# Second-block experts: wide expert swapped to place 28, with four edits around routing, constants and norm vectors

## The chip, the cores and the metric

The kernel runs on one core of one Trainium2 chip. The metric is the device time of one execution in microseconds; shown is the median of several executions. A profile of one more execution gives the trace. All times within it count from its first instruction.

## The reference

A sequence of 256 tokens of width 1024 passes two blocks, each a mixer with a residual and then a layer of experts with another. The first block's experts choose their tokens (16 experts, 32 tokens each). The change lies in and around the second block's experts. There each token chooses: four groups of eight experts, the best group by a softmax, in it the two best experts:

```python
top_logit, top_local = lax.top_k(e_logits, EXPERT_TOPK)       # 2 of 8, in the chosen group
expert = g_sel[:, None] * EXPERTS_PER_GROUP + top_local       # 0..31
hid = silu(xb @ gate[e]) * (xb @ up[e]);  y += weight * (hid @ down[e])
```

256 tokens with two experts each make 512 places for 32 experts, 16 on average; an expert may get any number. Each expert has a gate and an up matrix of 1024 x 256 and a down matrix of 256 x 1024, 1 MB each in float32. Before the experts stands a layer norm (ln1), after them a residual and another (ln2).

## The kernel before

The work runs as one program on five engines; a scheduler orders each engine's instructions by the order of the source and a cost model, and inserts the waits. `issue_after(ins)` keeps an instruction behind another one of the same engine in that order, without a wait.

**Constants.** `setup2` and `load_s5` (L754 to L766) load the second block's constants (p2, cf2, p2s; 1.9 MB together) while the first block's experts run. They are issued from ScalarE's queue. All other large loads are issued by SP (`load1`, `w`, `prefetch2`). DMAs of the SP and ScalarE queues share a small set of completion counters, given out in turn; a DMA that takes a counter waits until the counter's earlier DMA has landed.

**Rows and routing.** `mix_out` (L1588) ends the mixer: the output rows of the two halves of tokens (a = 0, 1), the norm's statistics, the logits, then `split_rows`. It scales a half in place on VectorE, copies it, rounded and with its columns reordered, to x3h on ScalarE, and GpSimd subtracts the two into x3l. `route_rows` is the chain of some ten small VectorE instructions that picks the two experts; its result is the mask Mk. `moe2_route` counts Mk up by matmuls with a triangle, which gives each token's place in its expert (pos), builds one-hot matrices of 32 places per expert and gathers the tokens of the first eight experts by matmul with x3h and x3l. `weights` (run at the start of `moe2_experts`) works out the weight of each pick (Wt).

**A block of 32 places, and one more.** Every expert gets one block of 32 places. An expert with more than 32 tokens is found in `weights`; its number goes to a register (xid), and a 33rd block "x" computes its places 33 to 64, with weights loaded once more. If any other expert has more than 32, or this one more than 64, `moe2_overflow` loops over all experts.

**Loads and slots.** `order2` writes out the order of the loads: in groups of four experts, first the gates and ups, then the downs; before the last group the three of block "x". `prefetch2` takes for each load the slot of SBUF that came free first (`k.free2`, 18 slots); at the end of group 6 `restore3` takes three of them for the norm vectors and for the sum `k.pre`. The norm vectors (ln1 and ln2, weight and bias) are four DMAs from GpSimd's queue that repeat one row of 4 KB on 128 partitions each.

**The groups.** `moe2_experts` runs g = 0 to 7: `gate_up` of two experts at a time, `turn` (transposes), `down` of the four experts of the group before, `scatter` (adds their rows to the four accumulators in PSUM). Block "x" goes in group 7. The tiles yh and yl between `down` and `scatter` exist once. Then `finish` normalises and writes the output.

Of the kernel before, what the change touches and what calls it, by code (L numbers as in the profile page):

```python
# [11 lines left out]
I32 = mybir.dt.int32  # L12
# [741 lines left out]
def setup2(k):  # L754
    nc = k.nc
    n = k.s5o
    both = k.cp2.tile([P, n + k.io["cf2"].shape[1]], F32, tag="w0", bufs=1, name="p2")
    k.p2, k.c2f = both[:, 0:n], both[:, n:]
    nc.scalar.dma_start(k.p2, k.io["p2"][:, 0:n])
    nc.scalar.dma_start(k.c2f, k.io["cf2"])  # L760


def load_s5(k):
    n, m = k.s5o, k.io["p2"].shape[1]
    k.p2s = k.s5t.tile([P, m - n], F32, name="p2s")
    k.nc.scalar.dma_start(k.p2s, k.io["p2"][:, n:m])  # L766
# [821 lines left out]
def mix_out(k):  # L1588
# [15 lines left out]
    k.x3T = k.xg.tile([P, 8, S], F32, tag="xi2", bufs=2, name="x3T")  # L1604
    k.lg = k.xg.tile([P, 2, 36], F32, name="lg")
# [53 lines left out]
    norm_rows(1, st[1])  # L1659
    split_rows(0, st[0])  # L1660
    route = route_rows(k)
# [58 lines left out]
def prefetch2(k, n):  # L1720

    for _ in range(n):
        e, name = ORDER2[len(k.loaded2)]
        nk = 2 if name == "down" else 8
        k.slot2[e, name] = slot = k.free2.pop(0)
        k.loaded2[e, name] = t = k.slot_tile(*slot, (P, nk, 2048 // nk))
        src = k.io[f"expert_w_{name}_2"].rearrange("e (p k) n -> e p k n", p=P)
        if e == E2:
            if name == "gate":
                k.more2 = k.nc.values_load(k.xid[0:1, 0:1], engines=(mybir.EngineType.SP,), min_val=0, max_val=E2 - 1)  # L1730
            k.nc.sync.dma_start(t, src[bass.ds(k.more2, 1)].rearrange("e p k n -> p (e k) n"))
        else:
            k.nc.sync.dma_start(t, src[e])
# [68 lines left out]
def moe2_route(k):  # L1802
# [10 lines left out]
    for a in range(2):  # L1813
# [5 lines left out]
        V.tensor_tensor(oh[:, a], io32(k), k.pos[:, a, 0:8, None].to_broadcast([P, 8, C2]), OP.is_equal)  # L1819
        for kk in range(8):  # L1820
            sl = slice((kk % 2) * 256, (kk % 2 + 1) * 256)
            for x in (k.x3h, k.x3l):
                T.matmul(pg[kk // 2][:, sl], x[:, a, kk * P:(kk + 1) * P], oh[:, a].rearrange("p e c -> p (e c)"),
                         start=(a + kk % 2 == 0 and x is k.x3h), stop=(a == 1 and x is k.x3l), skip_group_check=True)
            if a:
                gathered2(k, xi, kk, pg[kk // 2][:, sl])
    k.wt2 = Wt.rearrange("p a g e -> p a (g e)")
    ps = k.pj()
    T.matmul(ps[:, 0:32], one, mk[:, 0, :], start=True, stop=False)
    T.matmul(ps[:, 0:32], one, mk[:, 1, :], start=False, stop=True)  # L1830

    def weights():
# [12 lines left out]
        io = k.c1("iota")  # L1845
        many, big = (pool.tile([P, n], F32, name=nm) for n, nm in ((E2, "many"), (2, "big2")))
        pick = V.scalar_tensor_tensor(many, ps[:, 0:32], C2 + 0.5, io[:, 0:E2], OP.is_gt, OP.mult)
        V.tensor_reduce(big[:, 0:1], many, AX.X, OP.max)
        k.xid = pool.tile([1, 1], I32, name="xid")
        V.tensor_scalar(k.xid, big[0:1, 0:1], -1.0, 0.0, OP.add, OP.max)  # L1850
        k.px, k.wx = (pool.tile([P, 2], F32, name=nm) for nm in ("px", "wx"))
        for a in range(2):
            for d, v in ((k.px, k.pos), (k.wx, k.wt2)):
                V.scalar_tensor_tensor(many, io[:, 0:E2], big[:, 0:1], v[:, a], OP.is_equal, OP.mult, accum_out=d[:, a:a + 1])
        V.tensor_scalar(many, io[:, 0:E2], big[:, 0:1], float(C2), OP.is_equal, OP.mult)
        V.scalar_tensor_tensor(many, ps[:, 0:32], -float(C2), many, OP.add, OP.subtract)
        V.tensor_reduce(big[:, 1:2], many, AX.X, OP.max)
        k.over = pool.tile([1, 1], I32, name="over")
        V.tensor_scalar(k.over, big[0:1, 1:2], 0.5, None, OP.is_gt)
        k.big2 = big  # L1860

    k.weights2 = weights


def moe2_overflow(k):
# [5 lines left out]
    over = nc.values_load(k.over[0:1, 0:1], min_val=0, max_val=1)  # L1871
# [4 lines left out]
    with tc.If(over > 0):  # L1876
        V.memset(k.rone, 1.0)
        kept = pool.tile([P, 2, E2], F32, name="kept")
        for a in range(2):
            V.scalar_tensor_tensor(kept[:, 0], k.c1("iota")[:, 0:E2], k.big2[:, 0:1], k.pos[:, a], OP.is_equal, OP.mult)  # L1880
# [63 lines left out]
def moe2_experts(k):  # L1944
# [31 lines left out]
    def gather_more():  # L1976
# [4 lines left out]
        for a in range(2):  # L1981
            V.tensor_tensor(oh["x"][:, a], k.c1("iota")[:, C2:2 * C2], k.px[:, a:a + 1].to_broadcast([P, C2]), OP.is_equal)
            G.tensor_scalar(ow["x"][:, a], oh["x"][:, a].bitcast(F32), k.wx[:, a:a + 1], None, OP.mult)
# [10 lines left out]
    def gate_up(r):  # L1994
        es = (2 * r, 2 * r + 1) if r != "x" else (E2,)
        ws = [loaded2(k, e, "gate", "up") for e in es]
        ps = k.mx()
        for kk in range(8):
            for i in range(2):
                for n, e in enumerate(es):  # L2000
                    x = xi["x"][:, kk, :] if e == E2 else xi[e // 8][:, kk, (e % 8) * C2:(e % 8 + 1) * C2]
                    T.matmul(ps[64 * i + 32 * n:64 * i + 32 * n + 32, 0:256], x, ws[n][i][:, kk, :], start=(kk == 0), stop=(kk == 7))  # L2002
        k.free2 += [k.slot2[e, n] for e in es for n in ("gate", "up")]
# [24 lines left out]
    def down(g):  # L2028
        o, ws, h = oT[g]
        es = range(4 * g, 4 * g + 4) if g != "x" else (E2,)  # L2030
# [8 lines left out]
        k.free2 += [k.slot2[e, "down"] for e in es]  # L2039
# [16 lines left out]
    k.weights2()  # L2056
    onehot(0)
    for g in range(NQ):
        o = g // 2
        if g % 2 == 0 and o + 1 < NQ // 2:  # L2060
            onehot(o + 1)
# [9 lines left out]
        if o + 1 < NQ // 2:  # L2071
# [12 lines left out]
    down(NQ - 2)  # L2084
    scatter(NQ - 2)
    turn(NQ - 1)
    down(NQ - 1)
# [9 lines left out]
def load_norm(k, slot, n):  # L2097

    t = k.slot_tile(*slot, (P, 2, D))
    src = k.io["lnv"]  # L2100
    for i in range(2):
        k.nc.gpsimd.dma_start(t[:, i, :], bass.AP(tensor=src.tensor, offset=src.offset + (2 * n + i) * D, ap=[[0, P], [1, D]]))
# [3 lines left out]
def restore3(k):  # L2106

    G = k.nc.gpsimd
    k.last2 = [k.free2.pop(0) for _ in range(3)]
    ln = load_norm(k, k.last2[0], 0)  # L2110
    k.pre = x = k.slot_tile(*k.last2[1], (P, 2, D))
    k.lnv2 = load_norm(k, k.last2[2], 1)
# [37 lines left out]
def body(ctx, tc, io, p2off, c2off):  # L2150
# [78 lines left out]
    ringg = k.pool("ringg", "right")  # L2229
    k.loaded2, k.slot2, k.free2 = {}, {}, [(ringg, i) for i in range(6)]  # L2230
# [50 lines left out]
```

## Time and profile before

| | |
|---|---|
| median of 3 executions | 1259.8 us (1259.2 to 1261.11) |
| profiled execution | 1256.34 us, span 1254.6 us |
| TensorE busy | 1039.7 us, 83% of the span |
| VectorE busy | 517.4 us, 41% |
| ScalarE busy | 370.3 us, 30% |
| GpSimd busy | 135.4 us, 11% |
| HBM read | 373.12 MB, 298 GB/s over the span |

The shares are averages over stages with different limits: where the DMA engines are full, TensorE waits for weights, and where TensorE is full, DMA has gaps. What an edit is worth is read from its own stage.

### The profile page before, as it was taken

Reading aid. Unit: us, or ns where it says so; the run is one execution under the profiler, and the core shown is the slowest. Engines: PE = TensorE matmul, PEld = TensorE weight load, DVE = VectorE, ACT = ScalarE, POOL = GpSimd, SP = SyncE. Lnnn points to the kernel's source line nnn. Section 1 sums busy time; section 2 is a strip of 40 time slices with the busy share of each in tenths; the row PEclk is TensorE's granted clock in tenths of the full one; section 3 lists DMA queues with packets and bytes.
Section 4 is the critical chain, followed back from the end, with each engine's and each line's share of the span. In section 5 each row is a group of like instructions: output and inputs, shape, how many; then the busy total and the mean of one; then the engine's idle time right before and its main releaser. Section 6 shows DMA issues by size and latency. Waiting matters only on the chain. (4 is left out here: it accounts for less than half of the span.)

```text
span 1254.6 us, 21023 instructions
## 1 busy us (share of the span) xinstructions
PE 1039.7 (83%) x8986; PEld 718.3 (57%) x8986; DVE 517.4 (41%) x1034; ACT 370.3 (30%) x634; POOL 135.4 (11%) x134
## 2 busy tenths in 40 slices
PE   8889997777668777767689999999999979666775
PEld 7889874344214233312169998898999855333332
DVE  5595653102374000124047564686638552111114
ACT  5445632100000000200034565843433532111112
POOL 1351000010060000000001100112002210004101
PEclk9999998988779889987899999998999989888778
DMA  9723579999999999999973342242146659999994
GB/s 365 288 83 116 203 289 365 379 402 407 421 420 421 420 421 420 421 420 421 420 303 133 135 168 101 101 168 103 61 178 248 261 227 419 421 420 420 419 421 165
DMA packets 52949, 375.58 MB, mean 299 GB/s; under 512 B 5874, under 2 KB 6130, under 8 KB 8051
## 3 DMA queue, kind: packets, MB, share of 16 engines
q1 hardware_dynamic: 51842, 370.09, 73.6%
q10 hardware_dynamic: 432, 2.00, 0.5%
q0 software_dynamic: 576, 2.10, 0.4%
q8 instruction: 72, 1.18, 0.4%
q14 instruction: 27, 0.21, 0.0%
HBM read 373.12 MB, written 1.05 MB: 298 GB/s over the span
## 5 line engine op out<-in xcount | busy, mean ns | idle before, releaser
L692 PE MATMUL mx<-w,xin 128*32 128x512 f32 x1024 | 180.6, 662 | 61.3 <-DMA w<-in_w_expert_up_dram 45.9
L776 DVE TENSOR_TENSOR wl<-w,wh 128x1024 fp32r<-128x1024 f32 x116 | 148.3, 1281 | 76.0 <-ACT wh L775 75.6
L775 ACT CAST wh<-w 128x1024 fp32r<-128x1024 f32 x118 | 123.3, 1048 | 112.9 <-PE pj L793 63.6
L793 PE MATMUL pj<-x,wh 128*128 128x256 f32 x800 | 152.4, 289 | 1.2 <-ACT wh L775 0.7
L692 PEld LDWEIGHTS mx<-w,xin 128*32 128x32 f32 x1024 | 37.0, 115 | 181.0 <-DMA w<-in_w_expert_up_dram 82.5
L793 PEld LDWEIGHTS pj<-x,wh 128*128 128x128 f32 x800 | 126.4, 193 | 5.1 <-issue 2.3
L793 PE MATMUL pj<-x,wl 128*128 128x256 f32 x400 | 114.7, 287 | 0.2
L2002 PE MATMUL mx<-w,xi 128*32 128x256 f32 x1024 | 76.6, 404 | 38.4 <-DMA w<-in_expert_w_gate_dram 36.0
L719 PE MATMUL mx<-w,hT 128*32 128x256 f32 x1024 | 81.5, 472 | 17.4 <-DMA w<-in_w_expert_down_dram 9.2
L704 ACT ACTIVATE sg<-mx,rsl 64x512 f32<-64x512 f32 x16 | 10.9, 682 | 239.4 <-PE mx L692 237.2
L793 PEld LDWEIGHTS pj<-x,wl 128*128 128x128 f32 x400 | 77.3, 193 | 1.1 <-DVE wl L776 0.6
L2002 PEld LDWEIGHTS mx<-w,xi 128*32 128x32 f32 x1024 | 36.6, 115 | 70.6 <-issue 48.0
L705 DVE SCALAR_TENSOR_TENSOR sg<-sg,rsl,mx 64x512 f32<-64x512 f32 x16 | 12.0, 749 | 145.5 <-ACT sg L704 145.4
L719 PEld LDWEIGHTS mx<-w,hT 128*32 128x32 f32 x1024 | 37.9, 132 | 54.1 <-issue 20.6
L727 DVE COPY ysb<-mx 32x256 f32<-32x256 f32 x32 | 13.5, 423 | 112.4 <-ACT ysb L727 112.4
L807 PE MATMUL pj<-wh,hT 128*128 128x256 f32 x320 | 57.6, 281 | 0.0
L727 ACT COPY ysb<-mx 32x256 f32<-32x256 f32 x32 | 11.6, 362 | 141.5 <-PE mx L719 134.3
L807 PEld LDWEIGHTS pj<-wh,hT 128*128 128x128 f32 x320 | 49.1, 189 | 1.0 <-ACT osq L447 0.3
L2037 PE MATMUL mx<-w,hT 128*32 128x512 f32 x264 | 44.9, 633 | 0.5 <-ACT hT L2017 0.5
L807 PE MATMUL pj<-wl,hT 128*128 128x256 f32 x160 | 44.7, 279 | 0.0
L1704 DVE TENSOR_TENSOR sg<-sg,mx 64x256 f32<-64x256 f32 (+1 forms) x17 | 7.2, 423 | 87.9 <-ACT sg L1703 87.9
L1545 PE MATMUL mx<-y,wh 128*128 128x256 f32 x192 | 36.2, 288 | 1.5 <-DVE y L825 1.3
(606 smaller groups left out, 1836.8 us busy)
## 6 DMA issues: line engine op xcount, KB each, us to landing
w<-in_w_expert_gate_dram SPq DMA_DIRECT2D x64, 1024.0 KB, 14.9
w<-in_w_expert_up_dram SPq DMA_DIRECT2D x64, 1024.0 KB, 13.2
w<-in_w_expert_down_dram SPq DMA_DIRECT2D x64, 1024.0 KB, 13.7
w<-in_w_in_dram SPq DMA_DIRECT2D x43, 1024.0 KB, 5.0
w<-in_expert_w_gate_dram SPq DMA_DIRECT2D x33, 1024.0 KB, 19.9
w<-in_expert_w_up_dram SPq DMA_DIRECT2D x33, 1024.0 KB, 19.8
w<-in_expert_w_down_dram SPq DMA_DIRECT2D x33, 1024.0 KB, 19.8
w<-in_w_out_dram SPq DMA_DIRECT2D x8, 1024.0 KB, 4.8
```

The costliest lines, as they stand in the source:

```text
L692: last = T.matmul(ps1[32 * i:32 * i + 32, :], x, w[:, kk, 512 * (i % 2):512 * (i % 2) + 512], start=(j + kk == 0), stop=(j == 3 and kk == 1))
L704: A.activation(sg, ps1[0:64, :], AF.Silu, scale=k.rsl[:, e:e + 1])
L705: V.scalar_tensor_tensor(sg, sg, k.rsl[:, e:e + 1], ps1[64:128, :], OP.mult, OP.mult)
L719: last = T.matmul(ps3[32 * q:32 * q + 32, 0:256], hT[:, ft % 4, (ft // 4) * 32:(ft // 4) * 32 + 32], d[:, kk, q * 256:(q + 1) * 256], star ...
L727: done = (V.tensor_copy if q % 2 else A.copy)(ysb[r0:r0 + 32, q * 256:(q + 1) * 256], ps3[32 * q:32 * q + 32, 0:256])
L775: k.halved = k.nc.scalar.copy(h, src).ins
L776: eng.tensor_tensor(l, src, h.bitcast(F32), OP.subtract)
L793: T.matmul(ps[:, m * S:(m + 1) * S], u[:, kk, :], v[:, kk, :], start=(kk + i == 0), stop=(kk == 7 and i == 2))
L807: T.matmul(ps[:, a * S:(a + 1) * S], u[:, 4 * kh + kk, a * P:(a + 1) * P], v[:, kk, :], start=(kh + a + kk + i == 0), stop=(kh + a == 2 an ...
L1545: T.matmul(pu[:, m * S:(m + 1) * S], u[:, kk, m * P:(m + 1) * P], v[:, kk, :], start=(kk + n == 0), stop=(kk == 3 and n == 2))
L2002: T.matmul(ps[64 * i + 32 * n:64 * i + 32 * n + 32, 0:256], x, ws[n][i][:, kk, :], start=(kk == 0), stop=(kk == 7))
L2037: T.matmul(py[q][32 * i:32 * i + 32, :], h[:, j, 32 * i:32 * i + 32], w[i][:, j, 512 * q:512 * q + 512], start=(j == 0), stop=(j == 1))
```

## The change

1. The three loads of constants are issued from GpSimd's queue.
2. `split_rows` writes the scaled rows, already reordered, to a tile of their own (x3w), for the first half on VectorE, for the second on ScalarE; the copy to x3h is then contiguous, and the subtract to x3l is on VectorE, for the second half behind its picks. `route(1)` stands ahead of `split_rows(1)`.
3. The instructions of `weights` come behind the one-hots, those of the next one-hots behind the gathered tokens; the first columns of the second gather move behind `gate_up(1)`.
4. The four norm vectors are loaded as four rows of 4 KB (`load_norms`, at the end of group 5, when the three slots are taken too) and spread on 128 partitions by eight matmuls with four rows and eight copies on ScalarE (`spread_norm`).
5. The expert with more than 32 tokens, if it is one of 8 to 31, changes places with the expert at place 28: `swap2` exchanges the two columns in pos, in the numbers of the experts and in Wt. Experts 8 to 31 are loaded by their numbers, one register load on SP for each. Block "x" uses the weights of place 28, so the loads are 96 and not 99. Its `gate_up` still opens group 7; its `down` and `scatter` go behind `turn(7)`.

```diff
 def setup2(k):
-    nc.scalar.dma_start(k.p2, k.io["p2"][:, 0:n])
-    nc.scalar.dma_start(k.c2f, k.io["cf2"])
+    nc.gpsimd.dma_start(k.p2, k.io["p2"][:, 0:n])
+    nc.gpsimd.dma_start(k.c2f, k.io["cf2"])
 def load_s5(k):
-    k.nc.scalar.dma_start(k.p2s, k.io["p2"][:, n:m])
+    k.nc.gpsimd.dma_start(k.p2s, k.io["p2"][:, n:m])
...
     def split_rows(a, st):
-        x = k.x3[:, a, :]
-        V.tensor_scalar(x, x, st[:, 1:2], st[:, 4:5], OP.add, OP.mult)
+        x, hi, lo = k.x3[:, a, :], k.x3h[:, a, :], k.x3l[:, a, :]
+        whole = k.x3w[:, a, :]
+        if a:
+            V.tensor_tensor(st[:, 7:8], st[:, 1:2], st[:, 4:5], OP.mult)
+            A.activation(by_row(whole), turned(x), AF.Identity, bias=st[:, 7:8], scale=st[:, 4:5])
+        else:
+            V.tensor_scalar(by_row(whole), turned(x), st[:, 1:2], st[:, 4:5], OP.add, OP.mult)
         with k.tc.issue_after(k.rows3.ins):
-            A.copy(by_row(k.x3h[:, a, :]), turned(x))
-        return G.tensor_tensor(by_row(k.x3l[:, a, :]), turned(x), by_row(k.x3h[:, a, :]).bitcast(F32), OP.subtract)
+            A.copy(hi, whole)
+        with k.tc.issue_after(k.picks2[a].ins) if a else nullcontext():
+            V.tensor_tensor(lo, whole, hi.bitcast(F32), OP.subtract)
...
     with k.tc.issue_after(k.picks2[0].ins):
         logits(1, st[1])
+    route(1)
     split_rows(1, st[1])
-    route(1)
...
+NSET, WIDE = 8, E2 - 4
 def order2():
-        if g == E2 // 4 - 1:
-            yield from ((E2, n) for n in ("gate", "up", "down"))
...
-        if e == E2:
+        if e >= NSET:
             if name == "gate":
-                k.more2 = k.nc.values_load(k.xid[0:1, 0:1], engines=(mybir.EngineType.SP,), min_val=0, max_val=E2 - 1)
-            k.nc.sync.dma_start(t, src[bass.ds(k.more2, 1)].rearrange("e p k n -> p (e k) n"))
+                with k.tc.issue_after(k.loads2.ins):
+                    k.at2[e] = k.nc.values_load(k.xid[0:1, e:e + 1], engines=(mybir.EngineType.SP,), min_val=0, max_val=E2 - 1)
+            k.loads2 = k.nc.sync.dma_start(t, src[bass.ds(k.at2[e], 1)].rearrange("e p k n -> p (e k) n"))
         else:
-            k.nc.sync.dma_start(t, src[e])
+            k.loads2 = k.nc.sync.dma_start(t, src[e])
...
+        V.scalar_tensor_tensor(many[:, NSET:], ps[:, NSET:32], C2 + 0.5, io[:, NSET:], OP.is_gt, OP.mult)
+        V.tensor_reduce(big[:, 0:1], many[:, NSET:], AX.X, OP.max)
+        k.any2 = big[:, 1:2]
+        V.tensor_scalar(k.any2, big[:, 0:1], 0.5, None, OP.is_gt)
+        V.tensor_scalar(k.sel2, io, big[:, 0:1], None, OP.is_equal)
+        for a in range(2):
+            swap2(k, k.pos[:, a], many)
+        V.tensor_scalar(at, io, -1.0, None, OP.add)
+        swap2(k, at, many)
+        V.tensor_copy(k.xid, at[0:1, :])
+        for a in range(2):
+            swap2(k, k.wt2[:, a], many)
...
+def swap2(k, v, scr):
+    nd = k.g.tile([P, 2], F32, tag="nd2", bufs=2, name="nd2")
+    V.scalar_tensor_tensor(scr, k.sel2, 1.0, v, OP.mult, OP.mult, accum_out=nd[:, 0:1])
+    V.scalar_tensor_tensor(nd[:, 1:2], v[:, WIDE:WIDE + 1], k.any2, nd[:, 0:1], OP.mult, OP.subtract)
+    V.scalar_tensor_tensor(v, k.sel2, nd[:, 1:2], v, OP.mult, OP.add)
+    V.tensor_tensor(v[:, WIDE:WIDE + 1], v[:, WIDE:WIDE + 1], nd[:, 1:2], OP.subtract)
...
     def gate_up(r):
-        es = (2 * r, 2 * r + 1) if r != "x" else (E2,)
+        es = (2 * r, 2 * r + 1) if r != "x" else (WIDE,)
...
-    k.weights2()
+    with k.tc.issue_after(k.last_oh.ins):
+        k.weights2()
...
-        if g == NQ - 1:
-            down("x")
-        elif g:
+        if g:
             down(g - 1)
         gate_up(2 * g + 1)
+        if g == 0:
+            gather(1, 0)
...
+        if g == NQ - 3:
+            load_norms(k)
         if g == NQ - 2:
             gather_more()
             restore3(k)
-    scatter("x")
-    down(NQ - 2)
     scatter(NQ - 2)
     turn(NQ - 1)
+    down("x")
+    scatter("x")
     down(NQ - 1)
     scatter(NQ - 1)
...
+def load_norms(k):
+    k.last2 = [k.free2.pop(0) for _ in range(3)]
+    k.lnr = k.slot_tile(*k.last2[1], (4, D))
+    k.nc.gpsimd.dma_start(k.lnr, k.io["lnv"])
+def spread_norm(k, slot, n):
     t = k.slot_tile(*slot, (P, 2, D))
     for i in range(2):
-        k.nc.gpsimd.dma_start(t[:, i, :], bass.AP(tensor=src.tensor, offset=src.offset + (2 * n + i) * D, ap=[[0, P], [1, D]]))
+        row = k.c1("ident")[0:4, 2 * n + i:2 * n + i + 1].to_broadcast([4, P])
+        for q in range(2):
+            sl = slice(512 * q, 512 * q + 512)
+            ps = k.mx()
+            k.nc.tensor.matmul(ps, row, k.lnr[:, sl], start=True, stop=True)
+            k.nc.scalar.copy(t[:, i, sl], ps)
     return t
```

## Rows read from the trace of the kernel before

**Rows 1.** Page, part 2: tenths of busy time in 40 slices of 31.4 us.
```profile
DMA  9723579999999999999973342242146659999994
```
**Rows 2.** Windows: length; busy PE, PEld, DVE, ACT, POOL; PEclk, DMA share, GB/s.
```profile
245.00:250.00 5.00, 4.25 (x70) 2.73 (x72) 0.60 (x2) 0.00 (x0) 0.20 (x1) 1.00 0.59 205
250.00:255.00 5.00, 5.00 (x42) 3.10 (x36) 0.85 (x2) 0.72 (x2) 2.08 (x3) 1.00 0.94 314
...
1100.00:1125.00 25.00, 19.02 (x180) 10.38 (x184) 3.65 (x8) 3.73 (x8) 1.90 (x4) 0.86 1.01 421
1203.57:1242.00 38.43, 36.72 (x270) 16.01 (x270) 7.92 (x15) 8.83 (x19) 0.00 (x0) 0.90 0.77 321
```
**Rows 3.** Timeline of SP's issues, 225 to 260 us: start, duration, what.
```profile
236.84 0.33 SPq L184 DMA_DIRECT2D w<-in_w_expert_up_dram  x1
252.93 0.33 SPq L184 DMA_DIRECT2D w<-in_w_expert_gate_dram  x1
```
**Rows 4.** Waits of SP, 226 to 300 us: who waited for whom, total, times, longest.
```profile
SPq L184 <- DMA p<-in_p_dram: 15.7, 1, 15.7
```
**Rows 5.** Timeline of VectorE, 984 to 1048 us, routing; in brackets the idle time before.
```profile
997.83 0.80 DVE L1637 TENSOR_SCALAR x<-x,lnst 128x1024 f32<-128x1024 f32 x1
...
1002.10 2.86 DVE L1781 SCALAR_TENSOR_TENSOR r_o<-lg,r_gm,p 128x4 f32<-128x4 f32 x1
...
1010.90 2.86 DVE L1788 TENSOR_TENSOR r_hm<-r_rp,r_es 128x8 f32<-128x8 f32 x1
1013.79 0.25 DVE L1789 SCALAR_TENSOR_TENSOR Mk<-r_o,r_u,r_hm 128x32 f32<-128x32 f32 x1
...
1022.35 0.14 DVE L1859 TENSOR_SCALAR over<-big 1x1 int32<-1x1 f32 x1
```
**Rows 6.** Timeline of GpSimd in the routing (the second such row starts at 1010.88).
```profile
1002.10 2.85 POOL L1640 TENSOR_TENSOR x3l<-x,x3h 128x1024 fp32r<-128x1024 f32 x1 [20.38 <-ACT x3h L1639]
```
**Rows 7.** Timeline of SP's issues, 830 to 1175 us (x counts merged issues).
```profile
1023.79 0.33 SPq L1733 DMA_DIRECT2D w<-in_expert_w_gate_dram  x1
...
1030.10 0.45 SPq L1733 DMA_DIRECT2D w<-in_expert_w_gate_dram  x1
```
**Rows 8.** Windows of 2 us at the end, columns as in Rows 2.
```profile
1218.00:1220.00 2.00, 2.00 (x24) 0.96 (x20) 0.00 (x0) 0.00 (x0) 0.00 (x0) 0.50 1.01 422
...
1232.00:1234.00 2.00, 1.27 (x18) 0.48 (x10) 0.28 (x1) 0.38 (x1) 0.00 (x0) 1.00 0.41 172
1234.00:1236.00 2.00, 1.34 (x12) 0.67 (x16) 0.14 (x1) 0.37 (x1) 0.00 (x0) 1.00 0.09 37
```
**Rows 9.** Timeline of TensorE, 1195 to 1255 us.
```profile
1201.16 1.03 PE L2002 MATMUL mx<-w,xix 128*32 128x256 f32 x2 [6.29 <-DMA w<-in_expert_w_gate_dram]
1203.57 5.38 PE L2002 MATMUL mx<-w,xix 128*32 128x256 f32 x29 [1.38 <-DMA w<-in_expert_w_up_dram]
...
1241.49 0.40 PE L2053 MATMUL mx<-yl,oT 128*128 128x512 f32 x1
```
**Rows 10.** DMA issues: count, KB each, median us from issue to landing.
```profile
w<-in_lnv_dram POOLq DMA_DIRECT2D x4, 512.0 KB, 9.9
...
p<-in_p_dram ACTq DMA_DIRECT2D x1, 727.0 KB, 4.4
```
**Rows 11.** Page, part 5: groups of instructions, busy us, mean ns, idle before.
```profile
L776 DVE TENSOR_TENSOR wl<-w,wh 128x1024 fp32r<-128x1024 f32 x116 | 148.3, 1281 | 76.0 <-ACT wh L775 75.6
...
L2037 PE MATMUL mx<-w,hT 128*32 128x512 f32 x264 | 44.9, 633 | 0.5 <-ACT hT L2017 0.5
```
**Rows 12.** Timeline of ScalarE, 984 to 1048 us.
```profile
995.38 1.15 ACT L1622 ACTIVATE x3h<-x,lnst 128x1024 fp32r<-128x1024 f32 x1 [0.28 <-DVE lnst L1615]
...
999.96 2.06 ACT L1639 CAST x3h<-x 128x1024 fp32r<-128x1024 f32 x1
```
**Rows 13.** The line that loads the register: duration in ns, min/median/max, starts.
```profile
L1730 SPq TENSOR_LOAD <-xid x1: 465/465/465, 1018.5 to 1018.5; - x1
```
**Rows 14.** Waits of TensorE, 1050 to 1204 us.
```profile
PE mx L2002 <- DMA w<-in_expert_w_gate_dram: 42.3, 6, 10.2
```

More of the change, by code (lines that the diff above doesn't have):

```diff
@@ L1659, in mix_out @@
     norm_rows(1, st[1])
+    route = route_rows(k)
     split_rows(0, st[0])
-    route = route_rows(k)
     route(0)
@@ L1822, in moe2_route @@
             for x in (k.x3h, k.x3l):
-                T.matmul(pg[kk // 2][:, sl], x[:, a, kk * P:(kk + 1) * P], oh[:, a].rearrange("p e c -> p (e c)"),
+                last = T.matmul(pg[kk // 2][:, sl], x[:, a, kk * P:(kk + 1) * P], oh[:, a].rearrange("p e c -> p (e c)"),
                          start=(a + kk % 2 == 0 and x is k.x3h), stop=(a == 1 and x is k.x3l), skip_group_check=True)
             if a:
-                gathered2(k, xi, kk, pg[kk // 2][:, sl])
+                k.last_xi = gathered2(k, xi, kk, pg[kk // 2][:, sl]) or k.last_xi
     k.wt2 = Wt.rearrange("p a g e -> p a (g e)")
     ps = k.pj()
-    T.matmul(ps[:, 0:32], one, mk[:, 0, :], start=True, stop=False)
-    T.matmul(ps[:, 0:32], one, mk[:, 1, :], start=False, stop=True)
+    with k.tc.issue_after(last.ins):
+        T.matmul(ps[:, 0:32], one, mk[:, 0, :], start=True, stop=False)
+        T.matmul(ps[:, 0:32], one, mk[:, 1, :], start=False, stop=True)
     def weights():
@@ L1851, in weights @@
-        k.px, k.wx = (pool.tile([P, 2], F32, name=nm) for nm in ("px", "wx"))
-        for a in range(2):
[L1853 to L1857, printed above, removed]
+        io = k.c1("iota")[:, 0:E2]
@@ new lines, in weights @@
+        k.sel2, big = (pool.tile([P, n], F32, name=nm) for n, nm in ((E2, "sel2"), (3, "big2")))
+        k.kept = pool.tile([P, 2, E2], F32, name="kept")
+        many, at = k.kept[:, 0], k.kept[:, 1]
+        V.scalar_tensor_tensor(many[:, NSET:], ps[:, NSET:32], C2 + 0.5, io[:, NSET:], OP.is_gt, OP.mult)
[3 more added lines that the diff above has]
+        V.tensor_scalar(k.sel2, io, big[:, 0:1], None, OP.is_equal)
@@ L1870, in moe2_overflow @@
     ln = k.ln1
-    over = nc.values_load(k.over[0:1, 0:1], min_val=0, max_val=1)
+    with tc.issue_after(k.loads2.ins):
+        over = nc.values_load(k.over[0:1, 0:1], min_val=0, max_val=1)
     wg, wu = (k.io[n].rearrange("e (p k) n -> e p k n", p=P) for n in ("expert_w_gate_2", "expert_w_up_2"))
@@ L2029, in down @@
         o, ws, h = oT[g]
-        es = range(4 * g, 4 * g + 4) if g != "x" else (E2,)
+        es = range(4 * g, 4 * g + 4) if g != "x" else (WIDE,)
         w = [loaded2(k, e, "down")[0] for e in es]
@@ L2038, in down @@
                              start=(j == 0), stop=(j == 1))
-        k.free2 += [k.slot2[e, "down"] for e in es]
+        if g != "x":
+            k.free2 += [k.slot2[e, "down"] for e in es]
         yh = pool.tile([m, D], F32R, tag="yh2", bufs=1, name="yh2")
@@ L2060, in moe2_experts @@
         if g % 2 == 0 and o + 1 < NQ // 2:
-            onehot(o + 1)
+            with k.tc.issue_after(k.last_xi.ins):
+                onehot(o + 1)
         if g == NQ - 1:
@@ L2108, in restore3 @@
     G = k.nc.gpsimd
-    k.last2 = [k.free2.pop(0) for _ in range(3)]
-    ln = load_norm(k, k.last2[0], 0)
+    ln, k.lnv2 = (spread_norm(k, k.last2[2 * n], n) for n in range(2))
     k.pre = x = k.slot_tile(*k.last2[1], (P, 2, D))
-    k.lnv2 = load_norm(k, k.last2[2], 1)
     for a in range(2):
@@ L2229, in body @@
     ringg = k.pool("ringg", "right")
+    k.at2 = {}
     k.loaded2, k.slot2, k.free2 = {}, {}, [(ringg, i) for i in range(6)]
```

37 lines of the change are left out of this document (18 added, 19 removed).

## The prediction

> **What bounds the kernel now.** I read the page's slices first, then went to the stretches the edits touch with tables of windows, timelines and waits. The slices [rows 1] show two long runs in which the DMA engines are full: slices 6 to 19 (about 190 to 630 us, the first block's experts) and 32 to 38 (about 1004 to 1223 us, the second block's). Between them TensorE is the bound. So an edit is worth something only if it shortens one of the full runs, brings its start forward, or shortens what TensorE still does after the last load.
>
> First run: it has one hole. Between 245 and 255 us only 205 and 314 GB/s moved, where a full stretch moves 421 [rows 2]. SP issued nothing from 236.84 to 252.93 [rows 3], and its table of waits says what for: 15.7 us, until the constants' load p, issued by ScalarE, had landed [rows 4]. No slot and no weight was the last to come.
>
> Between the runs, the second block's routing is a chain of small VectorE instructions. Two of them take 2.86 us where their like take about 0.2; each begins when a 2.85 us subtract on GpSimd begins and ends with it [rows 5, 6]. The reader is to see that the subtract itself is needed late, but that it holds up VectorE.
>
> Second run: the first of the loads that keep the engines full is issued at 1023.79, when the first experts' matmuls have released slots [rows 7]. From there one load of 1 MB lands every 1,048,576 / 421,000 = 2.49 us [rows 2], and DMA stops at about 1235.8: the window 1232 to 1234 still moves 172 GB/s, the next 37 [rows 8]. TensorE waits for weights until 1203.57 and never again: from there to 1242.0 it is busy 36.7 of 38.4 us [rows 2, 9]. The tail is TensorE's, and DMA ends about 6 us ahead of it.
>
> **The change, part by part.** The profiled execution is 1256.3 us (span 1254.6); the median of the runs shown is 1259.8, 3.5 us above it. I take the differences from the trace and subtract them from the median.
>
> (1) Constants from GpSimd's queue. SP's loads no longer share a completion counter with them. What is lost in the hole is (5 x 421 - 5 x 205 + 5 x 421 - 5 x 314) KB, 1.6 MB or 3.8 us; that is the upper bound. The next loads still need slots that TensorE releases, at a time that the rows do not show, and a load carries data only some 2.6 us after its issue (p takes 4.4 us to land [rows 10], its 727 KB at the full rate are 1.8 of that), so a hole of a microsecond or two stays. Lower bound nothing, if the slots come no earlier than the counter did. I take 2.5 us, and it reaches the end of that run whole, because DMA sets the pace there. GpSimd's queue holds nothing urgent behind these three. A rule speaks against this edit: the Trainium skill ("SBUF — State Buffer", Who interferes with whom) says that a DMA issued from GpSimd can starve while VectorE runs in a two-port mode, and advises the ScalarE or SP queue. No row here shows it; VectorE is busy 1.45 us of these 10 [rows 2], so by that rule the constants would come at most 1.5 us later and the sum would stay.
>
> (2) Rows split on other engines, contiguous. Off GpSimd go both subtracts, and with them twice 2.86 - 0.2 = 5.3 us of the routing chain. Added on VectorE: a subtract of 128x1024 per half, 1.28 us by the row of its like [rows 11]; the first one lands in the chain, the second is issued behind the second half's picks and runs while TensorE gathers the first half. The first half's scaling now reads with a stride: between 0.80 us (plain, VectorE [rows 5]) and 2.06 us (strided, ScalarE [rows 12]); I take 1.3, mostly beside the transposes. ScalarE's copies fall from 2.06 to about 1.15 [rows 12], and it gets the second half's strided scaling, 2.06, in a wait. Moving the weights' exponentials behind the one-hots may cost ScalarE's evictions up to a microsecond. Together 5.3 - 1.3 - 0.5 = 3.5 us earlier for the first expert matmuls, so for the release of slots and for 1023.79. Bounds: 1 us (scaling and table loads in the chain) and 6.5 us (the subtracts all in gaps).
>
> (3) Numbers of the experts swapped; experts 8 to 31 loaded by a register. Some 24 more VectorE instructions of up to 0.25 us [rows 5] lengthen the chain that ended at 1022.35 [rows 5] by about 5 us. The load that needs the numbers first was issued at 1030.10 [rows 7], behind six others of which most were still in flight: nothing, and without that cover each microsecond of lateness is one of DMA. SP reads a register per expert: 0.47 us [rows 13], under 1 us with what follows, against three loads of 2.49: nothing.
>
> (4) The norm's vectors: four broadcasts of 512 KB [rows 10] go, 2.1 MB or 5.0 us of the full run, replaced by one load of 16 KB, eight matmuls of four rows (0.63 us each by the row of their shape [rows 11]) and eight copies of half of 1.15 us on ScalarE. Their cover is TensorE's wait of 6.3 us ahead of 1201.16 [rows 9]; on the path they would cost up to 5 us. GpSimd's sum of the residual moves behind them and is needed only at 1241. Three slots are taken a group earlier, 15 instead of 18 for 12 loads a group: the queue gets shallower, not empty. I take 5.0, at least 4.
>
> (5) Three loads fewer, 7.5 us of DMA. Here I do not give the kernel the whole sum. The extra block's matmuls come first in the last group, and their weights now are the first two loads of that group, at the very place in the row of loads at which the three extra loads stood: 5 us after the previous group's last. From there TensorE had 36.7 us of work, and it has it still. So TensorE can start its tail no earlier than (1), (2) and (4) allow; what (5) gives is what TensorE lost inside the tail. That is: 38.4 - 36.7 = 1.7 us of waits; the granted clock of 0.50, the 1.2 GHz level, in the window 1218 to 1220 [rows 8], some 1 to 1.5 us, which may come again where the extra block's down matmuls now stand; overlap of the last evictions. The extra block's first matmuls stay as slow as they are (5.4 us for 29, behind a wait of 6.3 [rows 9]). I take 3 us. Bounds: 5.5 us gained (tail at full rate throughout) and 2 us lost (the extra block's down and scatter now stand directly ahead of the last group's, with an eviction between them that nothing hides, and at half rate).
>
> Sum: 2.5 + 3.5 + 5.0 + 3.0 = 14.0 us. 1256.3 - 14.0 = 1242.3 for a profiled execution, 1259.8 - 14.0 = 1245.8 for the median; I say 1246.
>
> **The rivals.** (a) TensorE keeps up and the end follows the last load, as the removed bytes suggest: 2.5 + 3.5 + 12.5 = 18.5, 1241.3. For it: TensorE waited 42 us for weights from 1050 on [rows 14]. Against: its tail had no wait for weights after 1203.57 [rows 9].
> (b) The front gives nothing: slots hold SP until 253, and ScalarE's strided scaling and table loads take up what GpSimd's subtract leaves. Then 5.0 and 2 of the tail: 1252.8. For it: no row shows when the slots behind the hole came free, nor a strided scaling on VectorE.
> (c) The change does not save the loads in effect: the overflow loop runs for an expert of the first eight, which is never swapped. Reloading 32 experts is 32 x 3 x 2.49 = 239 us, about 1490 us. The routing worked out from the reference's own inputs puts 39 tokens on expert 16 and at most 28 on any other: hardly.
> (d) Slower: the numbers come late. SP is a queue, and everything behind expert 8's first load waits with it. The first load of the run lands about 5 us after 1023.79 [rows 7] (2.6 + 2.49, above), the five behind it 2.49 us each, so the one ahead of expert 8's at about 1041; issued up to 1036 it leaves hardly a gap, and each microsecond after that moves 72 loads. The gain is gone at 1036 + 14 = 1050, and at 1053 the kernel would take 1263. Against: the old chain ended at 1022.35 and only some 5 us are added to it, less 3.5.
>
> **Chances.** Forecast 0.58 (its own range 1242 to 1250), (a) 0.20, (b) 0.15, (c) 0.01, (d) 0.03; 0.03 for a change in the order of work elsewhere that cancels the gain. The range goes from 1238 ((a) with the upper bound of (2)) to 1253 ((b)). A measurement of this kernel can tell 0.2%, 2.5 us, from no change. Faster 0.93: forecast, (a) and (b); same 0.03; slower 0.04.
>
> **What the changed profile would show.** (1) no wait of SP for the constants, and over 350 GB/s on average between 245 and 255. (2) no VectorE instruction of 2.8 us in the routing; the start of the full run about 6 us earlier on the clock of the span, 3.5 of them from routing. (3) expert 8's load issued with loads still in flight. (4) no 2 MB on GpSimd's queue, TensorE's eight four-row matmuls inside a wait. (5) DMA ending about 10 us ahead of TensorE instead of 6, and TensorE's tail from the extra block's first matmuls about 35 us instead of 38. I am wrong if the tail shortens by much more (rival a) or grows, if the run of loads has a gap near expert 8, or if the routing's end moves by less than 1 us.

## The result

Six executions of the changed kernel took 1240.0 to 1252.1 us, median 1243.0, against 1259.5 before: ratio 0.988 [0.9845, 0.9914]. The forecast was 1246.0, range 1238 to 1253. With two later series it is 1243.7 over 18 executions, before 1258.6 over 61: 14.9 us less, where the sum of the prediction was 14.0. Rival (a), 1241.3, is about as near to these times; only the profile decides between them.

The profiled execution is the longest of the 18 (1252.08 us, span 1250.2), and what it lost lies ahead of the second block's experts. Between the first run's last load (638.3) and the mean of the first output row (1001.24) it took 362.9 us, before 355.2, two later profiles of the same kernel 357.3 and 354.7; TensorE's granted clock was 0.95 from 700 to 760 us and 0.88 from 760 to 820, where before had 1.00. No edit lies there. So I read times from the first row's mean on, as "behind the mean" (before: 995.13, L1615; after: 1001.24, L1616).

**First run.** Windows, the columns as in [rows 2], and the longest waits of SP from 226 to 300 us, both of the changed kernel:

```profile
245.00:250.00 5.00, 3.42 (x31) 0.88 (x24) 0.75 (x1) 0.68 (x1) 0.00 (x0) 1.00 1.02 423
250.00:255.00 5.00, 4.48 (x70) 2.65 (x72) 0.42 (x1) 0.18 (x1) 1.55 (x3) 1.00 1.01 423
```
```profile
SPq L184 <- PE mx L692: 26.5, 10, 9.2
SPq L184 <- DMA w<-in_w_expert_up_dram: 14.2, 2, 12.1
```

The hole is gone (205 and 314 GB/s in [rows 2]), and so is the wait for p [rows 4]; SP waits for slots that TensorE frees and for the loads of weights themselves. DMA issues and the one wait for p, after:

```profile
p<-in_p_dram POOLq DMA_DIRECT2D x1, 727.0 KB, 9.5
```
```profile
POOL ln L1694 <- DMA p<-in_p_dram: 8.0, 1, 8.0
```

From GpSimd's queue p takes 9.5 us to land, from ScalarE's 4.4 [rows 10], and only GpSimd's own copy waits for it. Between its issue and its landing the DMA engines were busy 0.76 of the time before, at 210 GB/s, and all of it after, at 417, so p now shares them with the weights. The rule of the Trainium skill weighed in the prediction ("SBUF — State Buffer", Who interferes with whom: such a load can starve) could explain 0.85 us of the 5.1 at most, for VectorE is busy no longer than that in the 9.5; no run separates the two, and nothing hung on it.

**Routing.** VectorE's timeline, after, and SP's issues:

```profile
1001.24 0.22 DVE L1616 TENSOR_SCALAR lnst<-lnst 128x1 f32<-128x1 f32 x1 [2.85 <-ACT x L1615]
...
1003.93 1.26 DVE L1643 TENSOR_SCALAR x3w<-x,lnst 128x1024 f32<-128x1024 f32 x1
...
1008.09 1.22 DVE L1647 TENSOR_TENSOR x3l<-x3w,x3h 128x1024 fp32r<-128x1024 f32 x1
1009.22 0.22 DVE L1791 SCALAR_TENSOR_TENSOR r_o<-lg,r_gm,p 128x4 f32<-128x4 f32 x1
...
1014.70 0.25 DVE L1799 SCALAR_TENSOR_TENSOR Mk<-r_o,r_u,r_hm 128x32 f32<-128x32 f32 x1
...
1027.34 0.16 DVE L1870 CAST xid<-kept 1x32 int32<-1x32 f32 x1
```
```profile
1025.86 0.33 SPq L1743 DMA_DIRECT2D w<-in_expert_w_gate_dram  x1
...
1031.16 0.36 SPq L1741 DMA_DIRECT2D w<-in_expert_w_gate_dram  x1
```

The instruction that took 2.86 us takes 0.22; the strided scaling takes 1.26 (I took 1.3). The instruction that makes the second half's mask starts 13.5 us behind the mean instead of 18.7 (1013.79 - 995.13), the first load of the second run leaves 1025.86 - 1001.24 = 24.6 behind it instead of 28.7 [rows 5, 7]: 4.0 us earlier (taken: 3.5). The numbers of the experts are written 26.1 behind the mean, and expert 8's load is issued at 1031.16 with the DMA engines full (share 1.01 from 1030 to 1040; 1040 to 1050 below): rival (d) did not come.

**Second run and tail.** Windows, TensorE's timeline, one group of its lines and all its waits from 1167 us to the end, after:

```profile
1040.00:1050.00 10.00, 10.00 (x106) 5.78 (x99) 2.63 (x5) 2.69 (x5) 0.06 (x1) 1.00 1.02 422
...
1180.00:1190.00 10.00, 10.00 (x41) 6.23 (x42) 1.66 (x5) 3.45 (x9) 0.00 (x0) 0.72 1.01 419
1190.00:1200.00 10.00, 10.00 (x34) 3.02 (x36) 0.00 (x0) 2.77 (x5) 2.00 (x1) 0.50 1.02 424
1215.00:1220.00 5.00, 4.87 (x38) 2.52 (x30) 1.93 (x3) 1.75 (x3) 0.00 (x0) 1.00 1.01 416
1220.00:1225.00 5.00, 5.00 (x69) 2.22 (x67) 0.85 (x2) 0.85 (x3) 0.00 (x0) 1.00 0.54 224
1225.00:1230.00 5.00, 5.00 (x17) 1.98 (x16) 1.47 (x2) 1.73 (x3) 0.00 (x0) 1.00 0.00 0
```
```profile
1166.69 1.03 PE L2031 MATMUL mx<-w,xi 128*32 128x256 f32 x2 [7.73 <-DMA w<-in_expert_w_gate_dram]
...
1183.52 7.99 PE L2147 MATMUL mx<-w,cf 4*128 4x512 f32 x10
1191.44 1.07 PE L2031 MATMUL mx<-w,xi 128*32 128x256 f32 x4
1192.44 5.48 PE L2147 MATMUL mx<-w,cf 4*128 4x512 f32 x6
1197.85 5.23 PE L2031 MATMUL mx<-w,xi 128*32 128x256 f32 x57
...
1204.85 3.00 PE L2031 MATMUL mx<-w,xix 128*32 128x256 f32 x26
...
1235.92 0.39 PE L2084 MATMUL mx<-yl,oT 128*128 128x512 f32 x1
```
```profile
L2147 PE MATMUL mx<-w,cf 4*128 4x512 f32 x16 | 13.5, 1017 | 0.0
```
```profile
PE mx L2031 <- DMA w<-in_expert_w_gate_dram: 7.7, 1, 7.7
PE mx L2045 <- DVE sg L1711: 0.7, 2, 0.5
```

The last load lands at 1225.3, 224.0 behind the mean and 16.7 earlier than before (240.7): all the bytes and the routing arrived there. But the last matmul ends 235.1 behind the mean, only 11.7 earlier, 11.1 us behind the last load instead of 6.1. The eight matmuls that spread the norm's vectors (L2147; the trace has two records for each, 16 in all) I took for 5 us in a wait. They are 13.5 us at a granted clock of 0.72 and then 0.50, the 1.2 GHz level, and they leave no wait behind them: TensorE's last wait for weights, the 7.7 us above, ends at 1166.69, and at the extra block's weights, where one stood before, there is none.

### The profile page after: what moved, and what is told of

It is laid out like the page before. It is cut to its first block, busy times and chain, and to the rows that moved or that the text cites. A ratio compares the mean times of both kernels' runs of the same rounds, so it can differ in the third digit from the quotient of the medians.

```text
span 1250.2 us, 21280 instructions
## 1 busy us (share of the span) xinstructions
PE 1053.3 (84%) x9002; PEld 729.8 (58%) x9002; DVE 516.3 (41%) x1055; ACT 375.1 (30%) x643; POOL 129.2 (10%) x132
## 5 line engine op out<-in xcount | busy, mean ns | idle before, releaser
L775 ACT CAST wh<-w 128x1024 fp32r<-128x1024 f32 x118 | 123.3, 1048 | 111.3 <-PE pj L793 62.2
L704 ACT ACTIVATE sg<-mx,rsl 64x512 f32<-64x512 f32 x16 | 10.9, 682 | 226.9 <-PE mx L692 224.7
L727 DVE COPY ysb<-mx 32x256 f32<-32x256 f32 x32 | 13.5, 423 | 117.1 <-ACT ysb L727 117.1
```

The costliest lines, as they stand in the source:

```text
L704: A.activation(sg, ps1[0:64, :], AF.Silu, scale=k.rsl[:, e:e + 1])
L727: done = (V.tensor_copy if q % 2 else A.copy)(ysb[r0:r0 + 32, q * 256:(q + 1) * 256], ps3[32 * q:32 * q + 32, 0:256])
L775: k.halved = k.nc.scalar.copy(h, src).ins
```

## The experiments

Each is the changed kernel with the edit shown. "Last load" is the landing of the last expert weights, "last matmul" its end, in the profile of that run; executions of the changed kernel alone spread over 12 us, and the intervals of the ratios reach 0.2 to 0.4% to either side, 2.5 to 5 us, more than the 0.2% that the prediction took for the least it could tell. So small differences are read from the profiles, and these have a spread too: in three profiles of the changed kernel the last load lies within 0.9 us, the last matmul within 2.1. A difference of 1 or 2 us between single profiles is not clear of that.

| run | median us (executions) | ratio to before [95%] | last load behind mean | last matmul behind mean | matmul behind load |
|---|---|---|---|---|---|
| before | 1258.6 (61) | 1 | 240.7 | 246.8 | 6.1 |
| changed, first | 1243.0 (6) | 0.9880 [0.9845, 0.9914] | 224.0 | 235.1 | 11.1 |
| again | 1245.5 (6) | 0.9882 [0.9852, 0.9912] | 223.2 | 237.1 | 14.0 |
| again2 | 1244.2 (6) | 0.9896 [0.9861, 0.9931] | 224.1 | 235.0 | 10.9 |
| const | 1247.3 (7) | 0.9907 [0.9873, 0.9941] | 225.2 | 236.0 | 10.8 |
| split | 1247.7 (12) | 0.9918 [0.9887, 0.9949] | 226.2 | 237.2 | 10.9 |
| bcast | 1245.8 (6) | 0.9888 [0.9868, 0.9908] | 229.0 | 237.4 | 8.5 |
| reload | 1243.8 (5) | 0.9868 [0.9848, 0.9889] | 230.6 | 236.7 | 6.0 |
| both | 1248.5 (10) | 0.9926 [0.9896, 0.9955] | 235.8 | 241.9 | 6.0 |
| early | 1242.8 (5) | 0.9867 [0.9848, 0.9886] | 223.2 | 231.9 | 8.7 |
| early_reload | 1245.9 (6) | 0.9896 [0.9866, 0.9926] | 230.5 | 236.5 | 6.0 |
| fill | 1240.7 (6) | 0.9848 [0.9809, 0.9888] | 224.2 | 231.9 | 7.7 |
| best | 1242.9 (6) | 0.9883 [0.9841, 0.9926] | 225.4 | 236.6 | 11.2 |
| best2 | 1239.0 (6) | 0.9832 [0.9800, 0.9864] | 223.1 | 229.2 | 6.1 |

**The changed kernel twice more (again, again2).**

> The changed kernel as it is, for a second profile. The profiled execution of it that was shown took 1252.1 us while its other executions took 1240.0 to 1243.8. Theory: what was lost in that one is TensorE's granted clock between 690 and 820 us (0.95 and 0.88 where before had 1.00), so another execution takes 1240 to 1244 and has a granted clock of 1.00 there. Rival: something the change itself delays ahead of 1000 us; then the mixing stage ends late in this profile too, at the same clock.

> The changed kernel as it is, once more, beside the two versions on the same chip: 1243 to 1246, the last matmul 235 to 237 us behind the first row's mean.

Between 640 and 990 us the clock in `again` was 1.00 but for 0.97, 0.94 and 0.97 in three windows, and the stretch took 357.3 us; in `again2` 354.7, as before (355.2). The same kernel took 362.9, 357.3 and 354.7 us there, so the excess of the first profile is that execution's and not the edits'; the lower clock goes with it. The 1240 to 1244 expected of `again` was missed (median 1245.5). The three profiles put the last matmul 235.1, 237.1 and 235.0 behind the mean, mean 235.7; this is the base below (last load: mean 223.8).

**Constants on ScalarE's queue again (const).**

```diff
-    nc.gpsimd.dma_start(k.p2, k.io["p2"][:, 0:n])
+    nc.scalar.dma_start(k.p2, k.io["p2"][:, 0:n])
...
```

> The changed kernel with the three loads of constants on ScalarE's queue again. The prediction's term (1): 2.5 us slower, bounds 0 and 3.8; the last load of the first run lands 2.5 us later. Theory after the first profiles: that load landed at 639.9 in before and at 637.9 to 639.1 in five profiles of kernels with the edit, so 0.8 to 2.0 us, and in the whole time 1 to 2 us; SP's wait for p comes back. Rival: nothing at all, the hole was a slot's and the mixing stage behind takes the rest.

Windows and SP's wait in this run:

```profile
245.00:250.00 5.00, 2.90 (x43) 1.75 (x44) 1.17 (x2) 0.68 (x1) 0.00 (x0) 1.00 0.49 205
250.00:255.00 5.00, 5.00 (x57) 3.54 (x50) 0.85 (x2) 0.73 (x2) 0.93 (x3) 1.00 0.74 243
```
```profile
SPq L184 <- DMA p<-in_p_dram: 16.9, 1, 16.9
```

The hole and the wait come back with the queue alone. In the traces of this run and of before, the load of weights that waited is counted on the same counter as p; in the changed kernel no load of weights shares one with the constants. What the hole costs is less sharp. The first run's last load lands at 640.5 here and at 639.9 in before; in the twelve kept profiles with the edit it lands at 634.9 to 640.6, mean 638.0. That is some 2 us, inside their spread, and the 3.7 us between the medians are inside the intervals. My term of 2.5 fits, but no run shows its size more closely.

**Rows split as before (split).**

```diff
+        V.tensor_scalar(x, x, st[:, 1:2], st[:, 4:5], OP.add, OP.mult)
...
-            A.copy(hi, whole)
+            A.copy(by_row(k.x3h[:, a, :]), turned(x))
...
-            V.tensor_tensor(lo, whole, hi.bitcast(F32), OP.subtract)
+        return G.tensor_tensor(by_row(k.x3l[:, a, :]), turned(x), by_row(k.x3h[:, a, :]).bitcast(F32), OP.subtract)
```

> The changed kernel with the rows split as before: scaled in place, copied with a stride, subtracted on GpSimd. The prediction's term (2): 3.5 us slower, bounds 1 and 6.5. Theory after the first profiles: in before the first expert matmuls end 23.3 us behind the first row's mean, in five profiles with the edit 18.0 to 18.8, so 4.5 to 5.3 us for the start of the second run; since TensorE waits for weights (DMA sets its pace) up to its last long row of work, all of it comes through: 4.5 to 5 us slower. Rival: the open tail of TensorE takes a part of it, 0 to 2 us.

VectorE's and GpSimd's timelines in this run:

```profile
1003.53 2.86 DVE L1785 SCALAR_TENSOR_TENSOR r_o<-lg,r_gm,p 128x4 f32<-128x4 f32 x1
```
```profile
1012.29 2.92 POOL L1641 TENSOR_TENSOR x3l<-x,x3h 128x1024 fp32r<-128x1024 f32 x1 [5.93 <-ACT x3h L1640]
```

Only the first subtract stalls VectorE again; the second, at 1012.29, now begins when VectorE has nothing to do until 1014.81. The first load of the second run leaves 26.9 us behind the mean instead of 24.6, and the last lands about 2.4 us later, not 4.5 to 5 (226.2, where the profiles of runs with this edit and as many bytes have 223.1 to 225.4); the median, less exact, is 4.1 higher. The gain of the routing as a whole is 4.8 us at the last load (before to `both`, whose loads are as many and as large: 240.67 - 235.84). By subtraction the other half belongs to the new order of edits 2 and 3; no run undoes that order alone.

**Broadcasts (bcast), three loads more (reload), both.**

```diff
-        if g == NQ - 3:
-            load_norms(k)
...
+    k.last2 = [k.free2.pop(0) for _ in range(3)]
-    ln, k.lnv2 = (spread_norm(k, k.last2[2 * n], n) for n in range(2))
+    ln = load_norm(k, k.last2[0], 0)
...
+    k.lnv2 = load_norm(k, k.last2[2], 1)
```

`load_norm` is the four broadcasts of before, and the slots are taken a group later again.

> The changed kernel with the norm's vectors broadcast by four DMAs of 512 KB on GpSimd's queue again, and without the matmuls that spread them; slots are taken a group later, as before. The prediction's step: 5.0 us slower (2.1 MB of the full run), the matmuls being hidden. Theory after the first look: the matmuls stand open, 13.5 us of TensorE between 1183.5 and 1198 at a granted clock of 0.5, and TensorE's row of work has no wait behind them, so taking them out gives the tail the 5 us back that the DMA takes: 0 to 1 us from the changed kernel.

```diff
+        if g == E2 // 4 - 1:
+            yield from ((E2, n) for n in ("gate", "up", "down"))
...
-        es = (2 * r, 2 * r + 1) if r != "x" else (WIDE,)
+        es = (2 * r, 2 * r + 1) if r != "x" else (E2,)
...
-        es = range(4 * g, 4 * g + 4) if g != "x" else (WIDE,)
+        es = range(4 * g, 4 * g + 4) if g != "x" else (E2,)
```

> The changed kernel with the extra block's three weights loaded a second time, by the expert's number, at the head of the last group: 99 loads again, 7.5 us more DMA, all else kept. In the changed kernel the last load lands 11.0 us ahead of TensorE's last matmul, before it was about 6. Theory (TensorE binds the tail): of the 7.5 us only what exceeds that slack comes through, 7.5 - 5 = 2.5 us slower than the changed kernel; the prediction's term for this part was 3.0. Rival (a), the end follows the last load: 7.5 us slower.

> Two undone together: the extra block's three loads come a second time (99 loads), and the norm's vectors by four broadcasts of 512 KB, no matmuls to spread them. Alone, the first left TensorE's last matmul 0.6 us later behind the routing than in the changed kernel (mean of two profiles), the second 1.3 us. Theory (behind the last wait for weights TensorE's row of work is the bound; each undo alone is swallowed by the slack of 5 to 8 us between last load and last matmul): together 12.5 us more DMA exceed the slack, the last matmul comes 6 us behind the last load, 6 us later than in the changed kernel, three times the sum of the two. Rival: the two add, 2 us later.

The last load moves by about what the bytes say (5.0, 7.5 and 12.5): 5.2, 6.9 and 12.1 us. The last matmul moves by 1.7, 1.0 and 6.2, of which only the last is clear of the spread. The first two fall into the distance between last load and last matmul, which shrinks from 11 to 8.5 and to 6.0; together they don't fit in. In `bcast`, without the spread's matmuls, the wait for the extra block's weights is there (6.79 us, until 1195.33), and from there to the last matmul are 35.6 us. 6.0 or 6.1 is the least distance in any of the profiles, and with both undone TensorE waits as it did before ([rows 9]: 6.29 and 1.38 us). TensorE's timeline in `both`:

```profile
1189.32 1.03 PE L2034 MATMUL mx<-w,xix 128*32 128x256 f32 x2 [7.32 <-DMA w<-in_expert_w_gate_dram]
1191.72 6.04 PE L2034 MATMUL mx<-w,xix 128*32 128x256 f32 x29 [1.37 <-DMA w<-in_expert_w_up_dram]
```

**The spread moved up (early), and with three loads more (early_reload).**

```diff
+        if g == NQ - 2:
+            k.spread.append(spread_norm(k, k.last2[2], 1))
         gate_up(2 * g + 1)
...
         if g == NQ - 3:
             load_norms(k)
+            k.spread = [spread_norm(k, k.last2[0], 0)]
...
-    ln, k.lnv2 = (spread_norm(k, k.last2[2 * n], n) for n in range(2))
+    ln, k.lnv2 = k.spread
```

`early_reload` adds the edit of `reload` to this.

> The changed kernel with the matmuls that spread the norm's vectors moved up: four behind the load of the 16 KB, four ahead of the second half of the next group, where TensorE waits for weights (7.7 us ahead of 1166.7). Theory: the 13.5 us leave TensorE's tail, which is then tied to the last load as before (last matmul some 6 us behind it instead of 11): 4 to 5 us faster than the changed kernel, about 1238. Rival: they were hidden where they stood, or the tail has another bound (rows turned, block x): no difference over 1 us.

> The version with the norm's spread moved up, and the extra block's three weights loaded a second time at the head of the last group (99 loads). In the changed kernel these loads cost 0.6 us at the last matmul, though they are 7.5 us of DMA. Theory: they were free there only because TensorE's row of work, lengthened by the open spread, was the bound; with the spread moved up the last matmul came 8.7 us behind the last load and can come no nearer than 6, so now 7.5 - 2.7 = 4.8 us show: about 1247 against 1242.8. Rival: the loads are free in themselves (they fit the gaps of the queue): no more than 1 us.

TensorE's timeline in `early`:

```profile
1159.37 0.59 PE L2031 MATMUL mx<-w,xi 128*32 128x256 f32 x2 [1.84 <-DMA w<-in_expert_w_gate_dram]
...
1165.99 2.84 PE L2150 MATMUL mx<-w,cf 4*128 4x512 f32 x6
...
1190.63 1.03 PE L2031 MATMUL mx<-w,xix 128*32 128x256 f32 x2 [7.34 <-DMA w<-in_expert_w_gate_dram]
...
1226.25 0.40 PE L2084 MATMUL mx<-yl,oT 128*128 128x512 f32 x1
```

Now TensorE waits for the extra block's weights (7.34 us), and the last matmul comes 3.8 us earlier behind the mean (231.9 against 235.7, the earliest of the three 235.0). The median is only 0.9 lower, not the 4 to 5 expected: 1.0 us is lost again behind the last matmul (14.9 us to the end of the span, 13.8 to 13.9 in the three base profiles), and the rest is within the intervals. With the spread moved there, the same three loads that were worth 1.0 us are worth 236.5 - 231.9 = 4.6 (expected: 4.8), 3.1 by the medians. From 1190.63 to the end are 36.0 us: the tail of about 35 that the prediction named, and it exceeds what the last eleven loads and 6 us more take, 27.3 + 6 = 33.3, by 2.7.

**A new order in the last group (fill, best, best2).**

```diff
         if g == NQ - 1:
+            turn(g - 1)
+            scatter(g - 2)
+            down(g - 1)
             gate_up("x")
...
```

This comes on top of `early`'s edit; the calls that stood further down are left out for this group.

> The version with the norm's spread moved up, and besides the last group's order changed: the transposes, scatter and down matmuls of the groups before stand ahead of the extra block's gate and up, where TensorE waited 7.3 us for their weights. Theory: TensorE's row of work behind that wait falls by some 5 us, from 36 to 31, and its last matmul comes 6 us behind the last load instead of 8.7: 2 to 3 us faster than the spread moved up alone, 3 to 6 us faster than the changed kernel. Rival: the down matmuls wait for the last weights of their group and push the extra block back by as much: no difference over 1 us from the spread moved up alone.

`best2` adds to this that expert 28's down weights are loaded third in their group, and

```diff
+        if g == NQ - 1:
+            down("x")
+            scatter(NQ - 2)
+            scatter("x")
         gate_up(2 * g + 1)
...
```

and `best`, run first, had the last group's down matmuls in another order besides:

```diff
-        for j in range(2):
-            for q in range(2):
-                for i in range(len(es)):
+        for i in range(len(es)):
+            for j in range(2):
+                for q in range(2):
```

> A version for speed: spread moved up and last group's order changed as in the run before, and further the extra block's down weights loaded third in the last group, its down matmuls and scatter ahead of the last pair's gate and up, and the last group's down matmuls expert by expert, so that only those of the last expert wait for the last load. Theory (the last load is now the bound, and what stands behind it counts): last matmul 3.5 us behind the last load instead of 7.7, 4 us faster than the run before, about 1236.5. Rival: evictions between the small matmuls, which nothing hides, eat it: no difference over 1 us.

> The version for speed of the run before with one thing taken back: the last group's down matmuls go round the four experts again instead of expert by expert. There the 32 records of them took 8.86 us, in the version with the last group's order changed 3.65. Theory (the order alone costs that): 3.7 us again, the last matmul 6 us behind the last load and 5.2 us earlier behind the routing than in the run before (231.4 instead of 236.6), the time some 5 us shorter than that run's profiled 1243.1, 1238, and 1 to 2 us below the version with the last group's order changed, since the extra block's down no longer stands behind the last load. Rival: the late last load or the clock stretched them; they take 6 to 9 us again.

`fill` brought the last matmul 1.0 us nearer to the last load and none nearer to the mean; its median is 2.1 below `early`, which the intervals don't separate, so its 2 to 3 us are not shown. `best` missed (1242.9 for 1236.5, its last matmul 4.7 us later behind the mean than `fill`'s), and not for either reason on record. The last group's down matmuls in `fill`, `best` and `best2`:

```profile
1218.51 3.65 PE L2067 MATMUL mx<-w,hT 128*32 128x512 f32 x30
```
```profile
1216.08 8.86 PE L2067 MATMUL mx<-w,hT 128*32 128x512 f32 x32 [0.46 <-ACT hT L2048]
```
```profile
1211.41 4.71 PE L2068 MATMUL mx<-w,hT 128*32 128x512 f32 x32 [0.46 <-ACT hT L2048]
```

The same 32 records (two are missing from `fill`'s) take 8.86 us expert by expert and 3.65 or 4.71 going round the four, at a granted clock of 1.00; `best` and `best2` differ in this order alone. Each expert's output lies in its own 32 of the 128 columns of TensorE. The Trainium skill ("TensorEngine Tiling (Array Packing)", Key Properties) says that tiles of the array operate independently and can load weights and multiply in parallel; the rows agree. Single records show it too: in `fill` four start within 0.03 us, one of each group of columns, and the next four some 0.43 us later; in `best` those of one expert also start 0.43 us apart, but the next expert's begin only half way through them. The 4.71 of `best2` is 3.65 and a wait of 1.06 inside the row: three experts start at 1211.41, the fourth at 1212.50, its weights having landed at 1212.46. `best2`, without `best`'s order, ends 229.2 behind the mean, 6.1 behind the last load: 1239.0 us, ratio to before 0.983, 4.7 us under the changed kernel's median of 1243.7. These 6.1 us are the last expert's own records, 3.6 us in one group of columns, and the scatter behind them.

## Why the prediction was right, and which of its steps failed

The time fell into the range, 0.5 to 3 us from the forecast in the three series (1243.0, 1245.5, 1244.2 for 1246), with the mechanism forecast for the tail: TensorE ends it, and the three loads are not worth their whole sum. One step failed, (4), and that it cost little is luck: of matmuls almost three times as long as priced about half fell into a wait, and another part is given back behind them.

(1) Right: the hole was the shared counter's, and went with the queue (const). For the term of 2.5 the first run's last load gives some 2, the medians 3.7, neither clear of the spread.

(2) and (3) Right, slightly small: 4.0 us at the first load, 4.8 at the last, for 3.5 + 0. The rows' split, with what it adds, is about 2.4 of it, not the whole 3.5 (split): behind the new order the second subtract holds nothing up. The numbers came not 5 us later but, behind the mean, earlier than the old chain's end.

(4) The step that failed: "eight matmuls of four rows (0.63 us each by the row of their shape [rows 11]) ... Their cover is TensorE's wait of 6.3 us ahead of 1201.16 [rows 9]; on the path they would cost up to 5 us." The bytes are right (5.2 us at the last load). But 633 ns [rows 11] is the mean length of one record of another matmul, and a matmul here has two: by the distance of records, one of four rows took 2 x 2.84 / 6 = 0.95 us at a granted clock near 1 (early, 0.97 from 1160 to 1170) and 2 x 5.48 / 6 = 1.83 at 0.50 (after). At the first price the eight would be 7.6 us; they were 13.5, and the rest goes with the lower clock. The cover was the wait named, at the extra block's weights, and with the matmuls gone it measures 7.34 us (early) and 6.79 (bcast): enough for 5 us, not for 13.5. So they ran past it by 13.5 - 7.3 = 6.2, and the extra block's first matmul starts 202.1 behind the mean (201.5, 203.5 and 201.4 in the three profiles; at 1202.70 in the first, where its weights had landed at 1197.93 and 1200.4) instead of 195.9 in `early`. From there to the last matmul it is 33.6 us in all three and 36.0 in `early`, where the extra block's 26 records behind the wait take 4.52 us instead of 3.00 (granted clock 0.66 from 1190 to 1200, after 0.92 from 1200 to 1210). What is left, 6.3 - 2.4, are the 3.9 us (3.8 in the table's rounded figures) that the move gives back. The term of nothing for TensorE should have been some 4 us.

(5) Right where (4) holds: with the spread moved up, the three loads gave 4.6 us, inside the bounds -2 and 5.5 and above the 3 taken. In the kernel as it is they gave 1.0, not clear of the spread, because the end was already TensorE's. (4) and (5) together gave 6.2 us instead of 8.0. The signs named for the tail came, but in part for another reason: DMA ended 11.1 us ahead of TensorE (10 were named), 2.4 of them through these matmuls (8.7 in `early`); from the extra block's first matmul to the last are 33.6 us (35 named), and with the wait back 36.0.

The sum by the profiles: 2 + 4.8 + 6.2 = 13. Behind the last matmul 0.9 to 2.2 us are lost again (span's end 12.7 us after it before, 13.6 to 14.9 in every changed profile; VectorE's and GpSimd's last instructions overlap otherwise; not tested). That leaves 11 to 12 us; 12.6 lie between the profiled execution before, 1256.3, and the changed median, 1243.7. The 14.9 between the medians is 3 to 4 more than the 11 to 12, which I can't assign; so that it is so close to the 14.0 of the prediction is in part luck.

Rival (a) falls: the end did not follow the last load, which came 16.7 us earlier for 11.7 at the last matmul. (b) falls with (1) and (2). For (c) and (d) nothing showed.

## What to carry to other kernels

Where two engines take turns as the bound, savings don't add: look up where the last wait for the other engine ends, and count for each edit only what lies ahead of that point, or what the distance at the end leaves over. Work added "in a wait" is priced from the distance of such instructions at the clock of that stretch, not from a mean record, and set against the length of the wait, since only what fits in is free: here 13.5 us against 7.3. To see what one part is worth, undo it alone, with another part, and with the bound removed: the three loads were worth 1.0 (within the spread), 4.5 (the step from `bcast` to `both`) and 4.6 us.

## What was not expected of the hardware

A float32 matmul with four rows and 512 columns cost 0.95 us at a granted clock of 0.97, all but the 2.4 GHz level, and 1.83 at 0.50, the 1.2 GHz level, and the granted clock was 0.72 and then 0.50 while TensorE was busy 20.0 of 20 us with the extra block's gather and these matmuls: here a full row of work in the profile did not mean the full clock.

Sixteen small matmuls (32 records) whose outputs lie in four groups of columns took 3.65 us when consecutive ones changed group, and 8.86 when four in a row stayed in one, both at a granted clock of 1.00.
